# Half-width products and a written order of products around a chunked recurrence

## The chip, the cores and the metric

The kernel runs on one core of a Trainium2 chip. The metric is the time of one execution on the device in microseconds. The kernel before took 880.96 us (median of 3 runs, 880.44 to 882.03).

The core's engines each take their instructions in the order in which they stand in the engine's queue: PE (matrix products; PEld is its loading of weights), DVE and ACT (elementwise work), POOL (here it starts DMA transfers), and SP (which issues DMA transfers).

## The reference

One block of a streaming encoder for a sequence of 512 frames, width 1024, batch 1. An input projection feeds two branches whose gated sum is added to x; a cross-attention into a memory of 256 frames and a gated convolutional feed-forward network (FFN) follow.

```python
h = rms_norm(x, norm_mix_g[l])
proj = h @ w_in[l] + b_in[l]                       # 1024 -> 4864 columns
y_a = rwkv7_branch(proj[..., :cb0], ...) @ w_branch_a[l]
y_b = rglru_branch(proj[..., cb0:cb1], proj[..., cb1:cb2], ...) @ w_branch_b[l]
merged = sigmoid(proj[..., cb2:cg1]) * y_a + sigmoid(proj[..., cg1:]) * y_b
x = x + merged @ w_mix_out[l]
x = x + cross_attention(rms_norm(x, norm_x_g[l]), rms_norm(mem, norm_mem_g[l]), w_cq[l], w_ckv[l], w_co[l])
x = x + conv_ffn(rms_norm(x, norm_ffn_g[l]), w_ffn_in[l], ffn_conv_w[l], ffn_conv_b[l], w_ffn_out[l])

# the recurrence of rwkv7_branch: 8 heads of 64, state S (64 x 64) of each head
sa = S_{t-1} a_t;  S_t = S_{t-1} * w_t + sa b_t^T + v_t k_t^T;  y_t = S_t r_t
# rglru_branch: a = exp(8 * gate_a * log_sigmoid(lam)); h_t = a_t h_{t-1} + xb_t gate_x_t sqrt(1 - a_t^2)
```

## The kernel before

**Dense products.** Activations lie as [128 channels x 512 frames]. Each fp32 product is made of three products of rounded operands: high by high, high by low, low by high (`mm3`, L179, L180, L181). Weights arrive as tiles of 128 x 1024, eight blocks of 128 x 128 each, from the SP queue into four buffers (`win_r` and the like); ACT casts the high part (L122) and DVE subtracts for the low part (L123); high and low parts have three buffers each. `dense` takes one block of 128 output channels through its input blocks, three products each, over all 512 columns: 24 products for an in_ps, q, co or mix block (8 input blocks), 12 for a yb or ya block. In all 1680 products have 512 columns: 38 in_ps blocks, 8 each of mix, q and co, 8 each of yb and ya. The FFN uses products of 256 columns; its weights, and those for the memory's keys, lie 32 elements into their buffer (`OFF`).

**The scores of the recurrence.** For each pair of heads (0 to 3), `sc` (L691) multiplies rows of AK by rows of KBt, which DVE makes for each half of the partitions e = 0, 1 (L653, L654). Then follow `zh` and `zo`, small products of a triangular inverse, with copies of Hs between them.

**The recurrence** works through 8 chunks of 64 frames. In each chunk (`chunk`), PE makes 16 products x (state by AK); DVE copies x to Xs (L863); 16 first products of y; 16 of u from Xs; ACT and DVE each copy one half of u into UV (L875, L876); 16 products vr bring the next chunk's v into rows; 16 products s from UV and KBr make the new state, which DVE multiplies by decays into Sn (L892) and adds into the next UV (L896; for chunk 0 a copy, L898); SP (L903) is the decayed state for the step after; then 16 last products of y, and four transposes kbr bring the next KBr, copied by ACT (L848). So x of one chunk waits for UV of the chunk before, which waits for Sn, which waits for s.

**The RG-LRU branch** runs at the same time: `px_gates` takes in_ps14 to in_ps17, makes a convolution on DVE (L950), two gate products of 512 columns in plain fp32 (ga, gx; L954, L956) and activations on ACT; `px_scan` makes exp, ln and exp on ACT, then gx, xb and the scan on DVE (L969 to L972). ACT loads a table between kinds of function (L264). in_ps18 to in_ps21 give the gelu gate of this branch. `group_norm` normalizes the recurrence's output in two halves of 256 frames and two pairs of heads: products gv (sums of squares, L175, L176) and gg (the gate, L931), where for the first half gv and gg share one bank of the tag `rg`; DVE reads gg last in L936.

**What sets the order.** The tile framework schedules each engine's instructions by a model of costs, due times and priorities. The recurrence has the highest priority (`high_priority(offset=1000000)`). Dense products of in_ps16 to in_ps19 are placed by that scheduler between the recurrence's small products. The FFN's weights are partly summed in memory ahead of time by DMA transfers from POOL's queue (dS, dOs); `NSUM` says how many of these sums go out behind the products of an in_ps block (`sum_behind`).

`yb2`, the high and low part of the RG-LRU branch's output, lies in a buffer that held one half of hT, the normalized input that the in_ps products read.

Of the kernel before, what the change touches and what calls it, by code (L numbers as in the profile page):

```python
# [10 lines left out]
F32R = mybir.dt.float32r  # L11
# [6 lines left out]
P = 128  # L18
T = 512
# [4 lines left out]
HD = 64  # L24
# [14 lines left out]
IN_ORDER = IN_RWKV + IN_REST  # L39


PV_LAYOUT = [
    ("b_in", 38), ("mu", 14), ("w0", 4), ("a0", 4), ("k_k", 4), ("k_a", 4), ("r_k", 4),
    ("lnx_g", 4), ("lnx_b", 4), ("cbw", 16), ("cbb", 4), ("b_ga", 4), ("b_gx", 4), ("lam", 4),
# [14 lines left out]
def hybrid_block_kernel(ctx: ExitStack, tc: tile.TileContext, xT_d, mT_d, pv_d, cst_d, win_d, wk_d, wv_d,  # L59
                        lup_d, gup_d, rga_d, rgx_d, wba_d, wbb_d, wmix_d, wq_d, wo_d, wfi_d, wfo_d, out_d):  # L60
    nc = tc.nc
    V, S, PE = nc.vector, nc.scalar, nc.tensor

    wp = ctx.enter_context(tc.tile_pool(name="wp", bufs=3))
    cp = ctx.enter_context(tc.tile_pool(name="cp", bufs=1))
    big = ctx.enter_context(tc.tile_pool(name="big", bufs=1))
# [32 lines left out]
    OFF = 32  # L99
# [78 lines left out]
    def mm3(ps, lh, ll, rh, rl, start, stop, **kw):  # L178
        first = PE.matmul(ps, lh, rh, start=start, stop=False, **kw)  # L179
        PE.matmul(ps, lh, rl, start=False, stop=False, **kw)  # L180
        PE.matmul(ps, ll, rh, start=False, stop=stop, **kw)  # L181
        return first
# [112 lines left out]
    with tc.tile_pool(name="p0", bufs=1, reuse_waits="tile") as p0:  # L295
# [6 lines left out]
        o = PV["nmem"][0]  # L302
# [548 lines left out]
    def pc_b(c):  # L851
        return PC[:, :, c].unsqueeze(2).to_broadcast([P, NPAIR, HD])

    def chunk(c, UV, KBr, SP):
        last = c == NC - 1
        nUV = nKB = None
# [20 lines left out]
        if not last:  # L877
            nUV = rows_v(c + 1)
            pss = ch_ps(f"s{c}", "s")
            for j in range(NPAIR):  # L880
                for e in range(2):
                    PE.matmul(pss[half[e], j * HD:(j + 1) * HD], KBr[:, j, half[e]], UV[:, e, j, :],
                              start=True, stop=True)
# [61 lines left out]
    def px_gates(b):  # L945
        ps = inproj(14 + b)
        xb = tp.tile([P, T], F32, tag="xb", name=f"xb{b}", bufs=2)
        S.activation(xb, ps, AF.Identity, scale=par("cbw", 12 + b), bias=cbias[:, b:b + 1])
        for k in range(1, 4):
            V.scalar_tensor_tensor(xb[:, k:], ps[:, 0:T - k], par("cbw", 4 * (3 - k) + b), xb[:, k:],  # L950
                                   ALU.mult, ALU.add)
        V.tensor_tensor(xb[:, 0:3], xb[:, 0:3], ccor[:, :, b], ALU.subtract)
        psa = rw_ps(f"ga{b}", prg, tag="rg")
        PE.matmul(psa, rg[:, 0, b, :], xb, start=True, stop=True)  # L954
        psx = rw_ps(f"gx{b}", prg, tag="rg")
        PE.matmul(psx, rg[:, 1, b, :], xb, start=True, stop=True)  # L956
# [25 lines left out]
    for i in IN_REST[NMID:]:  # L982
        if i < 18:
            pair.append(px_gates(i - 14))
            if len(pair) == 2:
                for p in pair:
                    px_scan(*p)
                pair = []
        elif i < 22:
            if i == 19:  # L990
                for jp in range(2):
                    group_norm(0, jp, rw_ps(f"gv0_{jp}", prg, "rg"), rw_ps(f"gg0_{jp}", prg, "rg"))
            py_block(i - 18)
        else:
            gate_block(i - 22)
# [6 lines left out]
    pch_ctx.close()  # L1002


    yb2 = big.tile([P, 2, 4, T], F32R, tag="act16_0", name="yb2")
    mB = big.tile([P, KB, T], F32, tag="act16_1", name="mB")
    for b in range(4):
        yb = YB[:, b, :]
        with tc.high_priority():
            S.copy(yb2[:, 0, b, :], yb)  # L1010
            V.tensor_tensor(yb2[:, 1, b, :], yb, yb2[:, 0, b, :].bitcast(F32), ALU.subtract)
# [14 lines left out]
    ua = Units(wba_d, "wba")  # L1026
    for m in range(KB):
        ga = pm.tile([P, T], F32, tag="ga", name=f"gta{m}", bufs=5)
        nc.sync.dma_start(ga, dG[m])
# [84 lines left out]
    vs = load_kv("V", 0)  # L1114
    split_kv(vs[:1])
    vs = vs[1:] + load_kv("V", 1)
    uq = Units(wq_d, "wq")

    def q_head(hd, nsum=2):
        q2 = pk.tile([P, 2, 2, T], F32R, tag="q2", name=f"q2_{hd}", bufs=2)  # L1120
# [77 lines left out]
    uo = Units(wo_d, "wo", order)  # L1198
# [369 lines left out]
```

## Time and profile before

| | |
|---|---|
| median of 3 runs | 880.96 us (880.44 to 882.03) |
| profiled execution | 880.53 us, span 878.7 us |
| mean granted TensorE clock | 0.997 |
| busy: PE, PEld, DVE, ACT, POOL | 865.9, 756.0, 677.0, 514.0, 132.5 us |
| in_ps products of 512 columns | 304 each of three lines |
| recurrence, first vr to the group norm's first gg | 272.79 to 326.46 us |
| mix | 389.82 to 433.77 us |
| q and the attention, co, to the FFN's first product | 433.77 to 551.62 us |

How to read it: a timeline row gives start and duration in us, the engine, the line of the kernel, the operation, its output and inputs, the tile, and how many such instructions are put together; a square bracket gives the idle time before and what ended it. A matmul's duration overlaps that of the next, so a stream's pace is read from start to start. A group row gives total busy time, mean duration in ns, then idle time before the group's instructions. A window row gives its bounds, its length, then busy time and number of instructions of PE, PEld, DVE, ACT and POOL, the granted clock of PE, the DMA share and GB/s.

### The profile page before, as it was taken

The page shows a single profiled execution, that of the slowest core. Times are in us where ns is not written, and L with a number is a line of the kernel's source. Part 1 is how long each engine was busy: PE and PEld are TensorE (multiplying, and loading weights), DVE is VectorE, ACT ScalarE, POOL GpSimd, SP SyncE. Part 2 cuts the span into 40 slices and gives each one's busy share as a digit, 9 for nine tenths or more (in the row PEclk, how much of TensorE's full clock was granted, in tenths as well). Part 3 has the DMA queues.
Part 4 walks back from the last instruction along what each step waited for, and adds up shares of the span by engine and source line. Part 5 has one row for each costly group of instructions (what it writes and reads, how often), then busy time and mean ns, then how long its engine had stood idle before and what let it go on. Part 6 is the DMA issues. An engine that isn't in the chain of part 4 may idle for free.

```text
span 878.7 us, 15954 instructions
## 1 busy us (share of the span) xinstructions
PE 865.9 (99%) x6204; PEld 756.0 (86%) x6204; DVE 677.0 (77%) x1096; ACT 514.0 (58%) x788; POOL 132.5 (15%) x163
## 2 busy tenths in 40 slices
PE   9999999999999999999999999999999999999996
PEld 8878878888877677888887778999999999999996
DVE  6796598777976776685575568799888888999674
ACT  7576676634438576334454357666666566767563
POOL 0102222021101022001122211111111111111100
PEclk9999999999999999999999999999999999999998
DMA  8879899678997379758887968999989999998963
GB/s 288 283 272 222 204 226 234 198 187 248 265 231 164 77 183 243 201 177 228 223 238 176 198 150 192 263 265 282 295 256 296 294 283 292 257 286 210 305 183 95
DMA packets 97562, 201.37 MB, mean 229 GB/s; under 512 B 19600, under 2 KB 30992, under 8 KB 97424
## 3 DMA queue, kind: packets, MB, share of 16 engines
q1 hardware_dynamic: 62240, 118.57, 40.9%
q0 software_dynamic: 25504, 67.38, 37.4%
q10 hardware_dynamic: 9744, 14.42, 4.9%
q8 instruction: 48, 0.79, 0.4%
q14 instruction: 26, 0.21, 0.1%
HBM read 188.54 MB, written 78.12 MB: 303 GB/s over the span
## 4 chain that ended last, share of the span: by engine, by line
PE 89%; DVE 6%; DMA 2%; ACT 2%; issue 1%; DVEq 0%; ACTq 0%; SPq 0%
PE in_ps L180 7%; PE in_ps L181 7%; PE in_ps L179 7%; PE fx_ps L179 4%; PE fx_ps L181 4%; PE fx_ps L180 4%; PE fyz_ps L181 3%; PE fyz_ps L179 3%; PE fyz_ps L180 3%; PE oyz_ps L179 2%; PE oyz_ps L180 2%; PE oyz_ps L181 2%; PE q_ps L180 2%; PE co_ps L180 2%; PE mix_ps L181 2%; PE co_ps L179 2%
## 5 line engine op out<-in xcount | busy, mean ns | idle before, releaser
L145 ACT CAST wfi_h<-wfi_r 128x1024 fp32r<-128x1024 f32 x77 | 80.9, 1050 | 69.9 <-PE fyz_ps L180 24.4
L180 PE MATMUL in_ps<-hT,win_h 128*128 128x512 f32 x304 | 121.1, 398 | 0.4 <-DVE hT L396 0.4
L181 PE MATMUL in_ps<-hT,win_l 128*128 128x512 f32 x304 | 121.4, 399 | 0.0
L179 PE MATMUL in_ps<-hT,win_h 128*128 128x512 f32 x304 | 120.2, 397 | 0.3 <-DVE pr L598 0.3
L494 POOL DMA_DIRECT2D dS<-in_wfi x66 | 66.7, 1028 | 298.8 <-PE in_ps L179 101.1
L146 DVE TENSOR_TENSOR wfi_l<-wfi_r,wfi_h 128x1024 fp32r<-128x1024 f32 x77 | 94.2, 1223 | 22.5 <-ACT wfi_h L145 22.4
L180 PEld LDWEIGHTS in_ps<-hT,win_h 128*128 128x128 f32 x304 | 57.1, 188 | 14.7 <-DVE hT L396 1.1
L179 PEld LDWEIGHTS in_ps<-hT,win_h 128*128 128x128 f32 x304 | 57.1, 188 | 13.5 <-DVE pr L598 0.7
L181 PEld LDWEIGHTS in_ps<-hT,win_l 128*128 128x128 f32 x304 | 57.1, 188 | 12.6 <-issue 0.7
L530 POOL DMA_DIRECT2D dOs<-in_wfo x54 | 39.8, 789 | 170.3 <-PE fx_ps L179 46.7
L123 DVE TENSOR_TENSOR win_l<-win_r,win_h 128x1024 fp32r<-128x1024 f32 x38 | 46.3, 1221 | 24.1 <-ACT win_h L122 20.7
L122 ACT CAST win_h<-win_r 128x1024 fp32r<-128x1024 f32 x38 | 39.9, 1049 | 42.6 <-PE in_ps L180 32.6
L1379 DVE TENSOR_TENSOR wfo_l<-wfo_r,wfo_h 128x1024 fp32r<-128x1024 f32 (+1 forms) x39 | 47.4, 1217 | 12.6 <-ACT wfo_h L1378 12.6
L1378 ACT CAST wfo_h<-wfo_r 128x1024 fp32r<-128x1024 f32 (+1 forms) x39 | 40.4, 1035 | 25.3 <-DMA wfo_r<-dOs 10.0
L181 PE MATMUL ox_ps<-go,wfo_l 128*128 128x256 f32 x176 | 48.7, 277 | 0.7 <-DVE wfo_l L1379 0.7
L181 PE MATMUL fyz_ps<-hq,wfi_l 128*128 128x256 f32 x176 | 48.7, 277 | 0.3 <-DVE wfi_l L146 0.3
L179 PE MATMUL fyz_ps<-hq,wfi_h 128*128 128x256 f32 x176 | 48.8, 277 | 0.1
L179 PE MATMUL fx_ps<-hr,wfi_h 128*128 128x256 f32 x176 | 48.7, 277 | 0.0
L179 PE MATMUL fx_ps<-hq,wfi_h 128*128 128x256 f32 x176 | 48.6, 276 | 0.0
L180 PE MATMUL fx_ps<-hq,wfi_h 128*128 128x256 f32 x176 | 48.6, 276 | 0.0
L181 PE MATMUL fx_ps<-hq,wfi_l 128*128 128x256 f32 x176 | 48.6, 276 | 0.0
L180 PE MATMUL fyz_ps<-hq,wfi_h 128*128 128x256 f32 x176 | 48.6, 276 | 0.0
(432 smaller groups left out, 2694.9 us busy)
## 6 DMA issues: line engine op xcount, KB each, us to landing
dS<-in_wfi POOLq DMA_DIRECT2D x66, 512.0 KB, 7.6
wfi_r<-dS SPq DMA_DIRECT2D x44, 512.0 KB, 6.6
win_r<-in_win SPq DMA_DIRECT2D x38, 512.0 KB, 5.3
wfi_r<-in_wfi SPq DMA_DIRECT2D x33, 512.0 KB, 6.2
dS<-dS POOLq DMA_DIRECT2D x22, 512.0 KB, 5.6
dOs<-in_wfo POOLq DMA_DIRECT2D x12, 512.0 KB, 8.4
wk_r<-in_wk SPq DMA_DIRECT2D x8, 512.0 KB, 5.2
wv_r<-in_wv SPq DMA_DIRECT2D x8, 512.0 KB, 4.7
```

What stands on the lines that cost most here:

```text
L122: casts.append(S.copy(hi[:, o:o + n], raw[:, o:o + n]))
L123: V.tensor_tensor(lo[:, o:o + n], raw[:, o:o + n], hi[:, o:o + n].bitcast(F32), ALU.subtract)
L145: S.copy(hi, raw)
L146: V.tensor_tensor(lo, raw, hi.bitcast(F32), ALU.subtract)
L179: first = PE.matmul(ps, lh, rh, start=start, stop=False, **kw)
L180: PE.matmul(ps, lh, rl, start=False, stop=False, **kw)
L181: PE.matmul(ps, ll, rh, start=False, stop=stop, **kw)
L494: return lambda: nc.gpsimd.dma_start(s(out), src, **kw)
L530: yield lambda k=k, w=w, src=src: nc.gpsimd.dma_start(dO[n, m][:, k * P:(k + w) * P], src, **kw)
L1378: S.copy(hi[:, :n], raw[:, :n])
L1379: V.tensor_tensor(lo[:, :n], raw[:, :n], hi[:, :n].bitcast(F32), ALU.subtract)
```

## The change

- `dense` makes each product of 512 columns as two products of 256, for each of the three parts in turn; the 1680 products become 3360. The weights of these stages get the 32-element offset.
- `Products` records each product and transpose by the name of the tile it writes; at the end, `arrange` chains them by dependencies without a semaphore in the order of the list `ORDER`. A name with a number (`in_ps18:6`) takes so many products of the tile, a name alone the rest. The list covers in_ps4 to co_ps1. In it the recurrence's chunks 0 to 7 have no dense product between them until the last chunk (6 halves of in_ps18 before u7, 12 after); the gate products ga2, gx2, ga3, gx3 stand behind chunks 0 to 3; each `sc` is one piece of 16; gv0_1 follows gg0_0.
- Weight sums: 7 fewer behind in_ps17, in_ps18 and in_ps19, and 7 behind the last s product of chunks 0 to 6.
- `yb2` takes the buffer of tag `x16` (it held KBt) in place of that of hT.

```diff
+ORDER = """
...
+in_ps16 in_ps17:4 zo0 zh16 in_ps17:10 zo16 in_ps17:10 vr0 in_ps17 x0 y0:8 kbr0 u0 vr1 s0 y0 kbr1 ga2 x1 y1:8 u1
+vr2 s1 y1 kbr2 gx2 x2 y2:8 u2 vr3 s2 y2 kbr3 ga3 x3 y3:8 u3 vr4 s3 y3 kbr4 gx3 x4 y4:8 u4 vr5 s4 y4 kbr5 x5 y5:8
+u5 vr6 s5 y5 kbr6 x6 y6:8 u6 vr7 s6 y6 kbr7 x7 y7:8 in_ps18:6 u7 in_ps18:12 y7 in_ps18 in_ps19:24 gv0_0 in_ps19
+gg0_0 gv0_1 in_ps20:24 gg0_1 in_ps20 in_ps21 gv1_0 gg1_0 gg1_1 yb_ps0:18 yb_ps1:10 gv1_1 yb_ps1:8 yb_ps0 yb_ps1
...
-    V, S, PE = nc.vector, nc.scalar, nc.tensor
+    V, S = nc.vector, nc.scalar
+
+    class Products:
+
+        def __init__(self):
+            self.made = {}
+
+        def log(self, out, ins):
+            self.made.setdefault(out.tensor.source_name, []).append(ins.ins)
+            return ins
+
+        def matmul(self, out, *args, **kw):
+            return self.log(out, nc.tensor.matmul(out, *args, **kw))
...
+        def arrange(self, order):
+
+            last = None
+            for item in order:
+                name, _, n = item.partition(":")
+                tiles = [t for t in self.made if t == name or t.startswith(name + "_")]
+                left = sorted((i for t in tiles for i in self.made[t]), key=lambda i: int(i.name.split("-")[1]))
+                take = left[:int(n)] if n else left
+                for t in tiles:
+                    self.made[t] = [i for i in self.made[t] if i not in take]
+                for i in take:
+                    if last is not None:
+                        tc.add_manual_dep(i, last.name, mybir.DependencyInfo(
+                            mybir.DependencyClass.NoSync, mybir.DependencyReason.DATA), reason="order of products")
+                    last = i
+
+    PE = Products()
...
     def dense(ps, units, rhs, nkb, nsum=0):
 
+        n = min(ps.shape[-1], T // 2)
         for kb in range(nkb):
             wh, wl = units.next()
             rh, rl = rhs(kb)
-            ins = mm3(ps, wh, wl, rh, rl, kb == 0, kb == nkb - 1)
+            for o in range(0, ps.shape[-1], n):
+                ins = mm3(ps[:, o:o + n], wh, wl, rh[:, o:o + n], rl[:, o:o + n],
+                          kb == 0 and o == 0, kb == nkb - 1, skip_group_check=o > 0)
             if kb * nsum % nkb < nsum:
                 sum_behind(ins)
         return ins
...
-    uin = Units(win_d, "win")
+    uin = Units(win_d, "win", at=OFF)
...
-            37: 1, 17: 4, 18: 5, 19: 5, 20: 2, 21: 1}
+            37: 1, 17: 2, 18: 2, 19: 3, 20: 2, 21: 1}
...
+            paces.append(ins)
...
+            if i == 17:
+                for ins in paces:
+                    sum_behind(ins)
...
-    yb2 = big.tile([P, 2, 4, T], F32R, tag="act16_0", name="yb2")
+    yb2 = big.tile([P, 2, 4, T], F32R, tag="x16", name="yb2")
...
-    ub = Units(wbb_d, "wbb")
+    ub = Units(wbb_d, "wbb", at=OFF)
...
+    PE.arrange(ORDER)
```

Three places show how instructions move. On PE, around the fifth chunk of the recurrence before (in_ps are dense products, the others those of the chunks):

```order
L882 MATMUL s_2658<-UV_2570,KBr_2599 64x64 x8
L887 MATMUL y_2625<-BZ,UV_2570 64x64 x8
L835 MATMUL vr_2723<-cst,vT 64x64 x8
L181 MATMUL in_ps_3314<-hT_0_87,win_l_3318 128x512
L179 MATMUL in_ps_3314<-hT_0_87,win_h_3317 128x512
L860 MATMUL x_2690<-UV_2646,AK 64x64
L867 MATMUL y_2701<-AK,UV_2646 64x64
L180 MATMUL in_ps_3314<-hT_1_88,win_h_3317 128x512
L860 MATMUL x_2690<-UV_2646,AK 64x64 x7
L867 MATMUL y_2701<-AK,UV_2646 64x64 x7
```

The same place in the changed kernel (all products are recorded at L94 and transposes at L97):

```order
L94 MATMUL s_3234<-UV_3146,KBr_3175 64x64 x8
L94 MATMUL y_3201<-BZ,UV_3146 64x64 x8
L97 MATMUL kbr_3252<-cst,KBt 128x128 x4
L94 MATMUL x_3266<-UV_3222,AK 64x64 x8
L94 MATMUL y_3277<-AK,UV_3222 64x64 x8
```

Between s and the next x stood y, vr and dense products; now y and the transposes kbr stand there, and nothing of in_ps.

On DVE, in chunk 6 of the changed kernel, from Xs to the next chunk's UV (L921 is the copy to Xs, L934 that of u, L951 Sn, L955 the next UV; L1028 to L1031 are the RG-LRU branch's gx, xb and scan):

```order
L921 COPY Xs_3351<-x_3342 128x256
L1030 TENSOR_TENSOR xb_4023<-xb_4023,gx_4034 128x512
L1028 SCALAR_TENSOR_TENSOR gx_4108<-ga_4107,gx_4108 128x512
L934 COPY UV_3298<-u_1_3363 64x256
L1031 SCALAR_TENSOR_TENSOR YB<-ga_4033,xb_4023 128x512
L1029 MEMSET gx_4108 128x1
L1030 TENSOR_TENSOR xb_4097<-xb_4097,gx_4108 128x512
L951 TENSOR_TENSOR Sn_3410<-s_3386,PC 128x256
L1031 SCALAR_TENSOR_TENSOR YB<-ga_4107,xb_4097 128x512
L955 TENSOR_TENSOR UV_3374<-Sn_3410,SP_3338 64x256 x2
```

Before, the same instructions of this branch stood one chunk's copies apart in nearly the same way (one xb product and one scan between Xs and the copy of u, a second scan between Sn and UV); what differs is that PE has no dense products to make meanwhile.

On PE, in the group norm, first before, then now:

```order
L931 MATMUL gg_0_3355<-sgx,gup 128x256 x2
L179 MATMUL in_ps_3395<-hT_0_87,win_h_3398 128x512
L180 MATMUL in_ps_3395<-hT_1_88,win_h_3398 128x512
L181 MATMUL in_ps_3395<-hT_0_87,win_l_3399 128x512
```
```order
L94 MATMUL gg_0_4197<-sgx,gup 128x256 x2
L94 MATMUL gv_1_4217<-gv_1_h,bonesr 128x512
L94 MATMUL gv_1_4217<-gv_1_l,bonesr 128x512
L94 MATMUL in_ps_4299<-hT_0_87,win_h_4302 128x256
```

Ten dense products stood between gg_0 and gv_1; now none does.

More of the change, by code (lines that the diff above doesn't have):

```diff
@@ L39 @@
 IN_ORDER = IN_RWKV + IN_REST
+ORDER = """
+in_ps4 in_ps5 in_ps0 in_ps1 in_ps8 in_ps9 psw0 psa0 ss0 in_ps6 in_ps7 in_ps2:6 sc0 in_ps2:12 psw1 psa1 in_ps2:18
+ss1 in_ps2 in_ps3 in_ps10:30 sc1 in_ps10 in_ps11 psw2 psa2 ss2 in_ps22 in_ps23 in_ps24:6 sc2 in_ps24 psw3 psa3
+ss3 in_ps25 in_ps26 in_ps27:30 sc3 in_ps27 in_ps28 bo0 in_ps29 bo1 in_ps30 bo2 in_ps31 bo3 in_ps32 in_ps33
+in_ps34 in_ps35 in_ps36 in_ps37 in_ps14 in_ps15:42 ga0 in_ps15 in_ps16:2 gx0 in_ps16:38 ga1 in_ps16:6 zh0 gx1
+in_ps16 in_ps17:4 zo0 zh16 in_ps17:10 zo16 in_ps17:10 vr0 in_ps17 x0 y0:8 kbr0 u0 vr1 s0 y0 kbr1 ga2 x1 y1:8 u1
+vr2 s1 y1 kbr2 gx2 x2 y2:8 u2 vr3 s2 y2 kbr3 ga3 x3 y3:8 u3 vr4 s3 y3 kbr4 gx3 x4 y4:8 u4 vr5 s4 y4 kbr5 x5 y5:8
+u5 vr6 s5 y5 kbr6 x6 y6:8 u6 vr7 s6 y6 kbr7 x7 y7:8 in_ps18:6 u7 in_ps18:12 y7 in_ps18 in_ps19:24 gv0_0 in_ps19
+gg0_0 gv0_1 in_ps20:24 gg0_1 in_ps20 in_ps21 gv1_0 gg1_0 gg1_1 yb_ps0:18 yb_ps1:10 gv1_1 yb_ps1:8 yb_ps0 yb_ps1
+yb_ps2 yb_ps3 yb_ps4 yb_ps5 yb_ps6 yb_ps7 ya_ps0 ya_ps1 ya_ps2 ya_ps3 ya_ps4 ya_ps5 ya_ps6 ya_ps7 mix_ps0
+mix_ps1 mix_ps2 mix_ps3 mix_ps4 mix_ps5 mix_ps6 mix_ps7 q_ps0_0:32 rxc_ps q_ps0_0 q_ps0_1 q_ps1_0:24 sc_ps0_0
+sc_ps0_1 q_ps1_0 q_ps1_1:4 sc_ps0_2 prT_ps0:2 q_ps1_1:8 sc_ps0_3 prT_ps0:2 q_ps1_1:18 prT_ps0 q_ps1_1:10 o_ps0
+q_ps1_1 o_ps1 q_ps2_0:4 sc_ps1_0 sc_ps1_1 q_ps2_0:16 sc_ps1_2 prT_ps1:2 sc_ps1_3 prT_ps1:2 q_ps2_0:16 prT_ps1
+q_ps2_0:10 o_ps2 q_ps2_0 q_ps2_1:18 o_ps3 q_ps2_1 q_ps3_0:16 sc_ps2_0 sc_ps2_1 q_ps3_0:14 sc_ps2_2 prT_ps2:2
+sc_ps2_3 prT_ps2:2 q_ps3_0:16 prT_ps2 q_ps3_0 q_ps3_1:16 o_ps4 q_ps3_1:16 o_ps5 q_ps3_1 co_ps0:16 sc_ps3_0
+sc_ps3_1 co_ps0:14 sc_ps3_2 prT_ps3:2 sc_ps3_3 prT_ps3:2 co_ps0:6 co_ps4:10 prT_ps3 co_ps4:10 o_ps6 co_ps4:12
+o_ps7 co_ps4:4 co_ps0:6 co_ps4:6 co_ps0 co_ps4 co_ps1
+""".split()
 PV_LAYOUT = [
@@ L61, in hybrid_block_kernel, with transpose @@
     nc = tc.nc
-    V, S, PE = nc.vector, nc.scalar, nc.tensor
+    V, S = nc.vector, nc.scalar
[7 more added lines that the diff above has]
+            return self.log(out, nc.tensor.matmul(out, *args, **kw))
+        def transpose(self, out, *args):
+            return self.log(out, nc.tensor.transpose(out, *args))
+        def arrange(self, order):
[13 more added lines that the diff above has]
+    PE = Products()
     wp = ctx.enter_context(tc.tile_pool(name="wp", bufs=3))
@@ L852, in pc_b @@
         return PC[:, :, c].unsqueeze(2).to_broadcast([P, NPAIR, HD])
+    paces = []
     def chunk(c, UV, KBr, SP):
@@ L881, in chunk @@
                 for e in range(2):
-                    PE.matmul(pss[half[e], j * HD:(j + 1) * HD], KBr[:, j, half[e]], UV[:, e, j, :],
-                              start=True, stop=True)
+                    ins = PE.matmul(pss[half[e], j * HD:(j + 1) * HD], KBr[:, j, half[e]], UV[:, e, j, :],
+                                    start=True, stop=True)
+            paces.append(ins)
         for j in range(NPAIR):
@@ L1116, in hybrid_block_kernel @@
     vs = vs[1:] + load_kv("V", 1)
-    uq = Units(wq_d, "wq")
+    uq = Units(wq_d, "wq", at=OFF)
     def q_head(hd, nsum=2):
@@ L1197, in hybrid_block_kernel @@
     order = [0, 4, 1, 5, 2, 6, 3, 7]
-    uo = Units(wo_d, "wo", order)
+    uo = Units(wo_d, "wo", order, at=OFF)
     for m in order:
```

4 lines of the change are left out of this document (2 added, 2 removed).

## The prediction

> **What bounds the kernel now.** I read the page's busy times first and then its chain of waits: TensorE (PE) works in 99% of the span and carries 89% of the chain that ends last. Time is therefore won or lost where the pace of PE's products changes, or where PE waits.
>
> ```profile
> PE 865.9 (99%) x6204; PEld 756.0 (86%) x6204; DVE 677.0 (77%) x1096; ACT 514.0 (58%) x788; POOL 132.5 (15%) x163
> PE 89%; DVE 6%; DMA 2%; ACT 2%; issue 1%; DVEq 0%; ACTq 0%; SPq 0%
> ```
>
> The 6% of DVE and 2% of ACT are mostly the recurrence. I read next the windows of the recurrence (272.79 to 326.46), the part of in_ps alone in it, and a purely dense stage, the mix.
>
> ```profile
> 272.79:326.46 53.67, 53.27 (x844) 38.88 (x843) 39.90 (x80) 38.30 (x72) 8.17 (x9) 1.00 0.58 134
> 272.79:326.46 53.67, 17.49 (x49) 8.09 (x48) 4.48 (x6) 2.23 (x3) 1.00 0.58 134
> 389.82:433.77 43.95, 43.95 (x194) 36.06 (x192) 25.39 (x32) 17.39 (x25) 7.47 (x8) 1.00 0.82 211
> ```
>
> PE shows no idle time in the first window, but 48 in_ps products and 2 of the group norm lie in it by program order (the second row counts 49 records, overlapping): 50 dense ones, at the mix's pace of 43.95/192 = 0.229 us worth 11.45 us. The recurrence itself, with four gate products, thus costs 53.67 - 11.45 = 42.2 us net. The granted clock is 1.00 in all these rows.
>
> **The change part by part.** (1) *Halves.* A product of 512 columns against one of 256, start to start, from the first and last row of a run of 45 and of a run of 51 intervals:
>
> ```profile
> 84.67 0.39 PE L179 MATMUL in_ps<-hT,win_h 128*128 128x512 f32 x1
> ...
> 94.97 0.39 PE L179 MATMUL in_ps<-hT,win_h 128*128 128x512 f32 x1
> ```
> ```profile
> 599.99 0.28 PE L179 MATMUL fyz_ps<-hq,wfi_h 128*128 128x256 f32 x1
> ...
> 605.77 0.28 PE L179 MATMUL fyz_ps<-hr,wfi_h 128*128 128x256 f32 x1
> ```
>
> 10.30/45 = 0.2289 and 5.78/51 = 0.1133; two halves take 0.2267, 2.1 ns less. 1680 products are split (912 of in_ps, 192 each of mix, q and co, 96 each of yb and ya): 1680 x 2.1 ns = **-3.5 us**. The FFN's rows already have the weights at the 32-element offset that the others get now, so I take its pace; the bounds are 0 (the smaller product gains only there) and -4. The number of weight loads doubles, and the FFN rows pay for the same number.
>
> The Trainium skill says otherwise: its page "TensorE: Matmul & The Clock Gate", section "Back-to-back issue gap", gives N/2.4 + 2.5 ns per product, so that halving would add 2.5 ns to each of 1680, an estimate of +4.2 us in place of -3.5. By that rule halves always cost; the two runs of rows above disagree with it (0.2267 against 0.2289).
>
> (2) *The recurrence in one piece.* One chunk before, on PE, and what DVE and ACT do for it:
>
> ```profile
> 298.97 0.69 PE L882 MATMUL s<-UV,KBr 128*64 128x64 f32 x16
> 299.58 0.67 PE L887 MATMUL y<-BZ,UV 64*64 64x64 f32 x14
> 300.19 1.12 PE L954 MATMUL ga<-xb,rg 128*128 128x512 f32 x2
> 301.24 0.69 PE L860 MATMUL x<-UV,AK 128*64 128x64 f32 x16
> 301.76 0.64 PE L867 MATMUL y<-AK,UV 128*64 128x64 f32 x16
> 302.32 0.33 PE L847 MATMUL kbr<-cst,KBt 128*128 128x128 f32 x1
> 302.58 0.68 PE L873 MATMUL u<-Xs,BZ 64*64 64x64 f32 x16
> 303.19 0.55 PE L847 MATMUL kbr<-cst,KBt 128*128 128x128 f32 x3
> 303.58 1.02 PE L956 MATMUL gx<-xb,rg 128*128 128x512 f32 x2
> 304.53 0.69 PE L882 MATMUL s<-UV,KBr 128*64 128x64 f32 x16
> ```
> ```profile
> 299.70 0.42 DVE L892 TENSOR_TENSOR Sn<-s,PC 128x256 f32<-128x256 f32 x1 [0.21 <-PE s L882]
> 300.16 0.87 DVE L896 TENSOR_TENSOR UV<-Sn,SP 64x256 f32<-64x256 f32 x2
> 301.06 0.87 DVE L903 TENSOR_TENSOR SP<-UV,PC 64x256 f32<-64x256 f32 x2
> 301.97 0.42 DVE L863 COPY Xs<-x 128x256 f32<-128x256 f32 x1
> 303.34 0.43 DVE L876 COPY UV<-u 64x256 f32<-64x256 f32 x1 [0.94 <-PE u L873]
> ```
>
> What is gained: dense products between small ones cost more than their 0.229 us.
>
> ```profile
> 276.34 0.50 PE L179 MATMUL in_ps<-hT,win_h 128*128 128x512 f32 x1
> 276.77 0.51 PE L873 MATMUL u<-Xs,BZ 64*64 64x64 f32 x10
> ```
>
> Here one occupies 0.43, so about 0.2 us goes with each place at which PE changes over; before has some 25 such places, 5 us. What is lost: the dense products had filled the waits. The chain without them, by the rows above: from s to the next x 0.69 + 0.42 + the first half of UV 0.43 and three gaps of 0.04 = 1.7 us, which y (0.61) and kbr (four, about 0.4) nearly fill, or 2.6 where a gate product (0.95) stands there too; from x to u 1.2 (0.69 + 0.42), or 1.8 where SP (0.87) stands before Xs on DVE; from u to s 1.25 (0.68 + 0.43, or vr's 0.61 behind u). That is 5.1 for a chunk with a gate product (0 to 3), 4.6 for 4 to 6, and 5.2 for the last, whose gaps hold 18 halves: 4 x 5.1 + 3 x 4.6 + 5.2 = 39.4. Less the halves (18 x 0.1133 = 2.0) and with the first vr (0.8), 38.2 net against 42.2, a gain of 4 if nothing else stood on DVE and ACT.
>
> But other work stands there, in order, with these lengths (groups of DVE, then ACT, within the recurrence):
>
> ```profile
> L972 DVE TENSOR_TENSOR_SCAN YB<-ga,xb 128x512 f32<-128x512 f32 x4 | 4.9, 1223 | 0.1
> L971 DVE TENSOR_TENSOR xb<-xb,gx 128x512 f32<-128x512 f32 x4 | 2.8, 692 | 0.2
> L969 DVE SCALAR_TENSOR_TENSOR gx<-ga,gx 128x512 f32<-128x512 f32 x4 | 2.8, 690 | 3.1 <-ACT gx L265 3.1
> L123 DVE TENSOR_TENSOR win_l<-win_r,win_h 128x1024 fp32r<-128x1024 f32 x2 | 2.4, 1220 | 0.0
> ```
> ```profile
> L264 ACT ACT_TABLE_LOAD x4 | 5.1, 1283 | 0.1
> L122 ACT CAST win_h<-win_r 128x1024 fp32r<-128x1024 f32 x2 | 2.1, 1049 | 0.3 <-PE in_ps L180 0.3
> ```
>
> I put the order of the changed DVE and ACT instructions beside these lengths, chunk by chunk, each starting when its inputs and its engine allow. Chunk 0: before the copy of u stand xb's product (0.69) and win_l (1.22), which waits for a table load (1.28) and the cast (1.05) on ACT; before Sn stand a scan (1.22) and an xb step: +2.5. Chunks 1 and 2: xb steps, and a tanh ahead of ACT's copy: +1.3. Chunks 3 to 5: +1.0. Chunk 6 again holds two xb products, two scans and a gx step around the copy of u and Sn, and a table load on ACT: +2.7. Sum +7.5. Lengths from x0 to the last y: 7.6, 5.8, 5.7, 5.3, 4.7, 5.3, 7.4, 5.2 = 47.0; less 2.0, with 0.8: 45.8 against 42.2, **+3.6**. Bounds: -4 when all of this slips beside the chain, +6 when a further scan and a table load (2.5) end last. I take the sum, because these engines take their instructions in order; laid out in the same way, before's stretch comes out within about 1 us of its trace.
>
> (3) *Group norm.* gv0_1 now follows gg0_0 at once, and both use one bank; gg0_0 is read until DVE's last step ends:
>
> ```profile
> 326.46 1.02 PE L931 MATMUL gg<-sgx,gup 128*128 128x256 f32 x4
> ```
> ```profile
> 328.64 0.69 DVE L936 TENSOR_TENSOR vT<-y,gg 128x512 f32<-128x512 f32 x1
> ```
>
> Before, ten dense products (2.3 us) fill the time to 329.33. Now PE waits: **+1.0** (bounds 0 and +2.2, the whole of 329.33 - 327.13). What is late is in_ps20 behind gv0_1 on PE's queue.
>
> (4) *Scores.* A set of 16 now runs in one piece and needs the rows of both halves at once:
>
> ```profile
> 133.50 0.69 DVE L653 TENSOR_TENSOR KBt<-kk,L 64x512 f32<-64x512 f32 x1
> 134.11 0.68 DVE L654 TENSOR_TENSOR KBt<-pk,L 64x512 f32<-64x512 f32 x1
> ```
> ```profile
> 117.88 0.50 PE L620 MATMUL psw<-pwa,lhi 128*128 128x512 f32 x1 [0.40 <-ACT BZ L698]
> 133.73 1.16 PE L691 MATMUL sc<-AK,KBt 64*128 64x128 f32 x8
> ```
>
> The eight products at 133.73 wait until 134.79 in the new form. Over four scores I take 2.0 of such waits, less psw's 0.4 and two changeovers of 0.2: **+1.2** (0 to +2.8). Small products zo behind copies of Hs, placed in the same way: **+0.3**.
>
> (5) *yb2 in another buffer.* The wait at yb goes with most of its changeover; gv1_1 now waits some 0.4 between the yb products:
>
> ```profile
> 345.95 0.50 PE L180 MATMUL yb_ps<-yb,wbb_h 128*128 128x512 f32 x1 [0.41 <-DVE yb L1011]
> ```
>
> **-0.2** (bounds -0.6 and +0.4). (6) *Weight sums.* Seven move from dense products to the s products of the chunks.
>
> ```profile
> dS<-in_wfi POOLq DMA_DIRECT2D x66, 512.0 KB, 7.6
> ```
>
> Their number is unchanged, the DMA share in the recurrence is 0.58, and what they feed, the FFN, starts 225 us after the recurrence: 0. Without that cover one landing of 7.6 us would be late. The attention's new order places products about as the trace has them: 0, within 1 either way.
>
> Sum: -3.5 + 3.6 + 1.0 + 1.2 + 0.3 - 0.2 = **+2.4**. The profiled execution took 880.53 (878.7 of span and 1.8 around it), so 882.9; the median of the runs is 0.43 higher: **883.4**.
>
> **The rivals.** *Slack on DVE and ACT takes half of the delay* (what (2) gains in changeovers pays the rest): recurrence about -0.1, all else as above, -1.3: 879.7. For it: before, DVE idles while it waits for u (0.94 us at 303.34). Against: in chunks 0 and 6 the queues before the copy are longer than such gaps. *The chain runs at its own pace*: recurrence -4, sum -5.2: 875.8. For it: DVE is busy 39.90 and ACT 38.30 of the window's 53.67 us, so that work spread evenly would just fit beside the chain; against: the chain's 39.4 is no longer than that, so nothing may stand in the wrong place. *Halves gain nothing outside the FFN* (slower): if a weight load or a bank's handover between halves takes back the 2.1 ns, which would decide in every dense stage, the sum is +5.9: 886.9. For it: two loads now stand where one did. Against: the FFN's pace. By the rule of the Trainium skill named above this case would come to an estimate of 891.1. That the change does not do what it says I exclude for PE: its listed order is the one the list of tiles asks for.
>
> **How the numbers follow.** Forecast 0.48, half of the delay 0.27, own pace 0.17, halves for nothing 0.08. Two per mille, 1.8 us, is about what the runs can tell from no change: 879.2 to 882.7. The own-pace case and the lowest parts of the half-delay one (0.08) are faster: 0.25; the rest of that and the lower end of the forecast (0.10) are the same: 0.29; what remains, 0.46, is slower. The forecast's own range, by the bounds of (2) to (4), is 881 to 887. Held to 8 in 10 with the own-pace case: 876.0 to 887.5.
>
> **What would show it.** Products of 256 in in_ps, mix, q and co start 0.1133 apart; the mix takes 43.5 us instead of 43.95. From x0 to the last y lie about 47 us, with PE waiting for the copies of u and for Sn in chunks 0 and 6, over 2 us each. About 1 us before gv0_1 is put down to DVE. The forecast is wrong if these waits stay under 1 us each (then it is near 876), or if the half products start over 0.1145 apart (then it is near 887).

## The result, and the profile after

The changed kernel takes 885.88 us (median of 4 runs, 885.61 to 887.02) against 880.7 for the kernel before beside it: ratio 1.0064, 95% interval 1.0051 to 1.0076, slower by 5.2 us by the medians. The profiled execution has a span of 885.2 us against 878.7; it was the slowest of the four, 1.1 us over the median, so the stages below add up to more than 5.2.

Of the changed kernel's page, the busy times and the engines of the chain that ended last:

```profile
PE 856.7 (97%) x7884; PEld 826.7 (93%) x7884; DVE 679.4 (77%) x1096; ACT 514.1 (58%) x788; POOL 132.5 (15%) x163
PE 72%; DVE 14%; ACT 6%; DMA 5%; issue 3%; DVEq 0%; ACTq 0%; SPq 0%
```

PE is busy 97% instead of 99%, and its part of the chain fell from 89% to 72%: most of what was added is waiting for DVE and ACT. The windows from the first vr to the first gg, of the mix, and of q, attention and co:

```profile
273.78:334.54 60.76, 52.98 (x915) 44.71 (x915) 41.15 (x82) 38.12 (x72) 11.65 (x13) 0.97 0.60 140
395.83:439.85 44.02, 43.80 (x387) 43.60 (x386) 25.51 (x33) 17.56 (x24) 7.47 (x8) 1.00 0.81 213
439.85:558.41 118.56, 116.53 (x954) 112.27 (x953) 79.86 (x171) 62.82 (x122) 21.23 (x23) 1.00 0.78 192
```

Before, PE was idle for 0.40 us of the first (53.27 busy of 53.67, which the prediction read as no idle time) and not at all in the other two; the third of before was

```profile
433.77:551.62 117.85, 117.85 (x569) 94.17 (x568) 78.88 (x171) 62.62 (x123) 21.27 (x23) 1.00 0.80 193
```

And within the mix, two rows with 174 half products between them:

```profile
414.01 0.39 PE L94 MATMUL mix_ps<-mg,wmix_h 128*128 128x256 f32 x2
...
433.73 0.39 PE L94 MATMUL mix_ps<-mg,wmix_h 128*128 128x256 f32 x2
```

19.72/174 = 0.1133: the halves run as the FFN's products do, 2.2 ns less for each former product (0.2289 - 0.2267). To see where time went, I take from each stage its dense products at their pace (0.2289 a product, 0.1133 a half) and compare the rest. From the first in_ps to the first vr the rest grew by 2.9 us, from there to gg by 4.5, from gg to yb (group norm) by 1.1, from yb to q by 0.6 (0.5 of it at the head of the mix, at a wait for its input), from q to the FFN by 1.6; the FFN and its end are 0.3 shorter, the start 0.1. That is +10.2, and -3.7 for the halves: +6.5, the difference of the spans.

The waits that carry it (PE's waits in the changed kernel; total, times, longest):

```profile
PE s L94 <- DVE UV L934: 2.7, 5, 0.9
PE x L94 <- DVE UV L955: 1.9, 1, 1.9
PE in_ps L94 <- DVE pr L654: 1.6, 1, 1.6
PE s L94 <- ACT UV L933: 1.5, 2, 0.8
PE sc L94 <- ACT kk L693: 1.2, 2, 0.6
```

The longest is in chunk 6. DVE's timeline there, and what PE shows:

```profile
314.01 0.43 DVE L934 COPY UV<-u 64x256 f32<-64x256 f32 x1
314.47 1.23 DVE L1031 TENSOR_TENSOR_SCAN YB<-ga,xb 128x512 f32<-128x512 f32 x1
...
315.75 0.69 DVE L1030 TENSOR_TENSOR xb<-xb,gx 128x512 f32<-128x512 f32 x1
316.48 0.42 DVE L951 TENSOR_TENSOR Sn<-s,PC 128x256 f32<-128x256 f32 x1
316.82 1.21 DVE L1031 TENSOR_TENSOR_SCAN YB<-ga,xb 128x512 f32<-128x512 f32 x1
317.95 0.84 DVE L955 TENSOR_TENSOR UV<-Sn,SP 64x256 f32<-64x256 f32 x2
```
```profile
318.40 1.07 PE L94 MATMUL x<-UV,AK 128*64 128x64 f32 x15 [1.93 <-DVE UV L955]
```

s is done at 315.3, yet Sn starts at 316.48, behind a scan and an xb step, and UV behind a second scan. Three windows from there on (the number before the DMA share is the granted clock):

```profile
318.00:320.00 2.00, 1.48 (x33) 1.26 (x33) 1.88 (x5) 0.00 (x0) 0.00 (x0) 0.96 1.04 158
320.00:322.00 2.00, 2.00 (x15) 1.78 (x16) 0.00 (x0) 0.00 (x0) 0.53 (x1) 0.50 1.02 253
322.00:324.00 2.00, 2.00 (x22) 1.88 (x20) 0.43 (x1) 0.36 (x1) 0.19 (x1) 0.69 0.83 209
```

After this wait PE's clock falls to half for 3.4 us (319.84 to 323.26), in the last chunk.

### The profile page after: what moved, and what is told of

Read it like the earlier page. It is cut to its first block, busy times and chain, and to the rows that moved or that the text cites. A ratio compares the mean times of both kernels' runs of the same rounds, so it can differ in the third digit from the quotient of the medians.

```text
span 885.2 us, 19309 instructions
## 1 busy us (share of the span) xinstructions
PE 856.7 (97%) x7884; PEld 826.7 (93%) x7884; DVE 679.4 (77%) x1096; ACT 514.1 (58%) x788; POOL 132.5 (15%) x163
## 4 chain that ended last, share of the span: by engine, by line
PE 72%; DVE 14%; ACT 6%; DMA 5%; issue 3%; DVEq 0%; ACTq 0%; SPq 0%
PE fx_ps L94 14%; PE in_ps L94 13%; PE fyz_ps L94 10%; PE ox_ps L94 6%; PE co_ps L94 5%; PE mix_ps L94 4%; PE q_ps L94 4%; PE oyz_ps L94 3%; PE yb_ps L94 2%; DVE win_l L176 2%; PE v_ps L94 2%; DMA wfo_r<-dOs 1%; PE o_ps L94 1%; PE k_ps L94 1%; PE sc_ps L94 1%
## 5 line engine op out<-in xcount | busy, mean ns | idle before, releaser
L94 PE MATMUL in_ps<-hT,win_h 128*128 128x256 f32 x1216 | 213.5, 280 | 2.0 <-DVE pr L654 1.6
L94 PEld LDWEIGHTS in_ps<-hT,win_h 128*128 128x128 f32 x1216 | 185.5, 188 | 5.7 <-DVE pr L654 1.8
L94 PE MATMUL in_ps<-hT,win_l 128*128 128x256 f32 x608 | 169.4, 279 | 0.6 <-DVE win_l L176 0.6
L94 PEld LDWEIGHTS in_ps<-hT,win_l 128*128 128x128 f32 x608 | 114.6, 189 | 1.9 <-DVE win_l L176 1.0
L94 PE MATMUL fx_ps<-hq,wfi_h 128*128 128x256 f32 x352 | 61.2, 276 | 0.0
L94 PE MATMUL fx_ps<-hr,wfi_h 128*128 128x256 f32 x352 | 61.1, 276 | 0.0
L94 PE MATMUL fyz_ps<-hq,wfi_h 128*128 128x256 f32 x352 | 61.1, 276 | 0.0
L94 PE MATMUL ox_ps<-go,wfo_h 128*128 128x256 f32 x352 | 60.0, 276 | 0.0
L1441 DVE TENSOR_TENSOR wfo_l<-wfo_r,wfo_h 128x1024 fp32r<-128x1024 f32 (+1 forms) x39 | 47.1, 1211 | 12.5 <-ACT wfo_h L1440 10.3
L94 PEld LDWEIGHTS fx_ps<-hq,wfi_h 128*128 128x128 f32 x352 | 53.2, 188 | 0.0
L94 PEld LDWEIGHTS fx_ps<-hr,wfi_h 128*128 128x128 f32 x352 | 53.0, 188 | 0.2 <-ACT sn L1376 0.2
L94 PEld LDWEIGHTS ox_ps<-go,wfo_h 128*128 128x128 f32 x352 | 53.0, 188 | 0.0
L94 PEld LDWEIGHTS fyz_ps<-hq,wfi_h 128*128 128x128 f32 x352 | 53.0, 188 | 0.0
L94 PE MATMUL ox_ps<-go,wfo_l 128*128 128x256 f32 x176 | 48.7, 277 | 0.7 <-DVE wfo_l L1441 0.7
L94 PE MATMUL fyz_ps<-hq,wfi_l 128*128 128x256 f32 x176 | 48.7, 277 | 0.6 <-DVE wfi_l L199 0.6
```

What stands on the lines that cost most here:

```text
L94: return self.log(out, nc.tensor.matmul(out, *args, **kw))
L1441: V.tensor_tensor(lo[:, :n], raw[:, :n], hi[:, :n].bitcast(F32), ALU.subtract)
```

## The experiments

Theory at the start: the halves gain about 3.7 us wherever they stand, and the written order loses more than that, in the recurrence (4.5), the group norm (1) and the attention (1.6). Ratios are to the kernel before, run beside each.

**Halves alone.** The kernel before with the new `dense` and the offset, no written order.

> The kernel before with only the half-width products and the weights' offset; the scheduler orders all products. Theory (halves gain 2.1 to 2.3 ns for each of 1680, the written order loses): 880.7 - 3.7 = 877, between 876 and 879. Rival (halves themselves bring the loss, by waits they make or by what the scheduler does with twice as many products): 883 or more.

904.61 us, ratio 1.0255 (1.0234 to 1.0276). The theory missed by 27.6 us. PE's waits in this run:

```profile
PE yb_ps L179 <- DVE mB L1021: 3.7, 1, 3.7
PE sc L694 <- DVE KBt L657: 2.9, 5, 0.9
PE in_ps L181 <- DVE win_l L123: 2.9, 5, 0.8
```

They lie in several of the mixed stages. The scheduler had remade the order of all engines for products of another size, so this run does not show the halves' own worth. It shows that the written order is not to be measured against the order of before: with halves and no written order the kernel is 19 us slower than with it.

**The written order with products of 512 columns** (`n = ps.shape[-1]`, counts of dense pieces halved).

> The changed kernel with its written order and paced sums, but products of 512 columns (the counts in the order halved, so that each piece holds the same work). Theory: the order alone costs what the change costs plus what the halves gain, 885.9 + 3.7 = 889.6, between 888.5 and 890.5. Rival (halves cost or give nothing here): 886 or less.

896.81 us, ratio 1.0178 (1.0159 to 1.0196): 7.2 over the theory. It reaches the first vr when the kernel before does (272.87 us against 272.79); then PE, DVE and ACT are in another relation, and this is the longest wait, with the clock behind it:

```profile
PE ga L93 <- DVE xb L1010: 4.5, 1, 4.5
```
```profile
280.00:286.00 6.00, 1.80 (x36) 1.43 (x36) 5.88 (x12) 2.94 (x6) 0.70 (x1) 0.86 0.72 218
286.00:292.00 6.00, 5.34 (x68) 3.61 (x70) 3.40 (x8) 2.12 (x4) 0.00 (x0) 0.57 0.00 0
```

More of the 7.2 us lies in the pace. In the mix, 84 products of 512 columns lie between these two rows:

```profile
411.75 0.62 PE L93 MATMUL mix_ps<-mg,wmix_h 128*128 128x512 f32 x2
...
431.21 0.62 PE L93 MATMUL mix_ps<-mg,wmix_h 128*128 128x512 f32 x2
```

19.46/84 = 0.2317, 2.8 ns more than the 0.2289 of before, worth 4.7 us for 1680 products. What the dense stages of this run have different from before is the weights' offset of 32 elements; the offset alone was not run. So by this run it isn't the offset that makes the halves faster: with the offset a full product takes longer, not less.

The parts of the change are not additive: order and size were fitted to each other.

**The recurrence left to the scheduler**, the rest of the written order kept:

```diff
-in_ps16 in_ps17:4 zo0 zh16 in_ps17:10 zo16 in_ps17:10 vr0 in_ps17 x0 y0:8 kbr0 ...
+in_ps16 in_ps17:4 zo0 zh16 in_ps17:10 zo16 in_ps17:10 [ vr0 in_ps17 x0 y0:8 kbr0 ...
...
-gg0_0 gv0_1 in_ps20:24 gg0_1 in_ps20 in_ps21 gv1_0 gg1_0 gg1_1 yb_ps0:18 ...
+gg0_0 gv0_1 in_ps20:24 gg0_1 in_ps20 in_ps21 gv1_0 gg1_0 gg1_1 ] yb_ps0:18 ...
```

(items between the brackets are counted but not chained).

> The changed kernel, but the order of products from the first vr to the last gg is left to the scheduler, which puts dense halves between the small products again. Theory (PE has nothing to do while it waits for DVE and ACT in the one-piece chunks, 4.5 us, and before gv0_1, 1 us): 885.9 - 5.5 = 880.4, between 879 and 882. Rival (the waits are set by DVE's and ACT's queues whatever PE does): 884 or more.

880.62 us, ratio 0.9998 (0.9987 to 1.0008). As the theory has it: vr to yb takes 47.4 us beside its dense products, against 47.1 before and 52.6 in the changed kernel. PE fills the time with halves. The run doesn't show this alone, for DVE's order moved with it: the last two scans stand in chunks 5 and 6, one each, where the changed kernel has both in chunk 6. But the kernel before has both in chunk 6 too, with dense products beside them.

**The attention left to the scheduler** (the list ends at mix_ps7).

> The changed kernel with its written order only up to the mix; q, the attention and co are left to the scheduler. Theory (the four new waits of 0.4 to 0.55 us at sc_ps and o_ps go): 885.9 - 1.6 = 884.3. Rival (those waits are moved work and cost nothing, or fewer changeovers pay for them): 885.5 to 886.5.

888.69 us, ratio 1.0077 (1.0062 to 1.0093): slower than the changed kernel, where both readings had it the same or faster. The intervals of the two overlap, but the stage itself tells them apart: from q to the FFN the rest is 33.8 us instead of 31.5. For halves the written order of the attention is better than the scheduler's; it is worse only beside what full products had.

**Halves in the order of before.** Written down for PE from the kernel before, counts of dense pieces doubled; sums and yb2's buffer as before.

> The kernel before (its sums and its buffer of yb2 too) with half-width products, and with its own order of products on PE written down: each dense piece has twice as many halves at the same place. Theory (halves gain about 2.2 ns for each of 1680 where PE never waits; the run with halves alone lost its time through the order that the scheduler made for them): 880.8 - 3.7 = 877, between 876 and 879.5, since a few waits on DVE may come earlier. Rival (halves cost by themselves in the mixed stages, so that before's order loses too): 883 or more.

886.09 us, ratio 1.0069 (1.0057 to 1.0081). The theory missed again. The largest wait, in the otherwise dense stage before the recurrence:

```profile
PE in_ps L124 <- DVE win_l L206: 2.5, 4, 0.9
```

DVE's order had moved: a cast of low weights stood two instructions of the triangular inverse later than its counterpart before. DVE in this run, then in the kernel before:

```profile
227.74 0.76 DVE L849 TENSOR_TENSOR zz<-Zt,Nm 128x576 f32<-128x576 f32 x1
228.42 1.22 DVE L206 TENSOR_TENSOR win_l<-win_r,win_h 128x1024 fp32r<-128x1024 f32 x1
```
```profile
225.81 0.71 DVE L763 TENSOR_TENSOR zz<-Zt,Nm 128x529 f32<-128x529 f32 x1
226.43 1.22 DVE L123 TENSOR_TENSOR win_l<-win_r,win_h 128x1024 fp32r<-128x1024 f32 x1
```

**gv0_1 apart from gg0_0**: `gg0_0 in_ps20:20 gv0_1 in_ps20:16 gg0_1`.

> The changed kernel with 20 halves of in_ps20 between gg0_0 and gv0_1 (and 16 in place of 24 before gg0_1). Theory (the wait of 0.97 us for the last reader of the shared bank goes, one changeover of 0.2 comes): 885.9 - 0.8 = 885.1. Rival (what follows gv0_1, gg0_1, then waits as long): 885.9.

884.42 us, ratio 1.0045 (1.0033 to 1.0057): 1.5 less than the changed kernel. The wait before gv0_1 is gone, and from gg to yb the rest falls from 5.5 to 4.3 us. The spans of the two profiled executions differ by more, 2.6 us, and the other 1.4 isn't the edit's: the same wait in chunk 6 stands here, but this time PE's clock stayed at 1.00 behind it, and the last chunk, from x to the start of the last y, took 4.64 us instead of 6.06.

```profile
319.37 1.07 PE L94 MATMUL x<-UV,AK 128*64 128x64 f32 x15 [1.93 <-DVE UV L955]
...
324.01 0.68 PE L94 MATMUL y<-BZ,UV 64*64 64x64 f32 x16
```

**Sums and buffer undone** (`NSUM` as before, no sums behind the chunks, yb2 in `act16_0`).

> The changed kernel with the weight sums counted as before (none behind the chunks) and yb2 in the buffer of hT again. Theory: the sums cost nothing (within 0.4) and the buffer's wait of 0.4 us at yb may come back: 885.9 to 886.4. Rival (seven sums in the recurrence slow its transfers, or the sums behind too few products come late for the FFN): 884.5 or less.

887.11 us, ratio 1.0075 (1.0063 to 1.0087). The wait for yb is back, with more than twice the time it had before (0.41):

```profile
PE yb_ps L94 <- DVE yb L1070: 1.0, 1, 1.0
```

The intervals of this run and of the changed kernel overlap. The buffer's wait is seen; sums and buffer are not told apart beyond that.

**Scans late.** The last two gx steps, and with them the xb steps and scans that need them, held behind the last chunk's copy of u:

```diff
-        V.scalar_tensor_tensor(gx, ga, 1.0, gx, ALU.add, ALU.mult)
+        ins = V.scalar_tensor_tensor(gx, ga, 1.0, gx, ALU.add, ALU.mult)
+        if b > 1:
+            tc.add_manual_dep(ins.ins, copied[-1].ins.name, mybir.DependencyInfo(
+                mybir.DependencyClass.NoSync, mybir.DependencyReason.DATA), reason="scan behind the chunks")
```

> The changed kernel with the last two gx steps, xb steps and scans of the RG-LRU branch held on DVE until the last chunk's copy of u. Theory (chunk 6 is 7.5 us long because two scans of 1.22 us and the steps before them stand ahead of the copy of u, Sn and the next UV): its length falls to about 5, the whole by 2.3 to 883.6, between 883 and 884.4. Rival (the table load on ACT, or the chain itself, sets chunk 6): 885.3 or more.

882.15 us, ratio 1.0021 (1.0012 to 1.003): 3.7 less, more than the 2.3 expected. Chunk 6, from x to x, falls from 7.51 to 5.29 us, as the theory has it:

```profile
309.66 0.98 PE L94 MATMUL x<-UV,AK 128*64 128x64 f32 x15
314.95 1.00 PE L94 MATMUL x<-UV,AK 128*64 128x64 f32 x15
...
319.51 0.68 PE L94 MATMUL y<-BZ,UV 64*64 64x64 f32 x16
```

The other 1.5 us is the last chunk: from x to the start of the last y 4.56 instead of 6.06 us, at a clock of 1.00:

```profile
316.00:318.00 2.00, 2.00 (x39) 1.74 (x33) 0.43 (x1) 0.00 (x0) 0.56 (x1) 1.00 0.95 122
```

So one idle piece of 1.93 us cost itself and 1.5 us more through the clock. That this is the clock, and not the scans' absence from the last chunk, is shown by the run with gv0_1 apart, which has the scans in their old place, the same wait, and 4.64 us at a clock of 1.00.

**Halves with every order of before.** As the run in PE's order of before, but DVE's and ACT's order is written down too, instruction by instruction; with that, only the width and the weights' offset differ.

> As the run with half-width products in the order of the kernel before, but the orders of DVE and ACT are written down too, instruction by instruction as in the kernel before; so the products' width is all that differs. Theory (the 886 of that run came from casts of weights that the scheduler put later on DVE once the products were halved, four waits of 0.5 to 0.9 us in a stage that is otherwise dense): the waits go and the halves' gain shows, 880.5 - 3.7 = 876.8, between 875.5 and 878.5. Rival (halves need the low part of the weights 0.23 us sooner, or cost elsewhere by themselves): 881 or more.

887.18 us, ratio 1.0067 (1.005 to 1.0083). The theory fell a third time: the waits for win_l are gone, and others stand in their place. In this kernel all instructions of ACT and DVE are recorded at L194, PE's products at L221. ACT, then PE, then three windows of this run; last, ACT's cast in the kernel before:

```profile
266.11 1.04 ACT L194 CAST win_h<-win_r 128x1024 fp32r<-128x1024 f32 x1 [2.33 <-PE in_ps L221]
```
```profile
267.81 1.18 PE L221 MATMUL zo<-BZ,Hs 32*32 32x32 f32 x60 [1.61 <-ACT Hs L194]
```
```profile
262.00:268.00 6.00, 4.38 (x87) 3.04 (x88) 1.51 (x2) 2.53 (x4) 0.00 (x0) 1.00 0.34 140
268.00:274.00 6.00, 6.00 (x188) 5.71 (x186) 3.03 (x6) 4.25 (x6) 1.14 (x1) 0.63 0.40 101
274.00:280.00 6.00, 6.00 (x59) 5.59 (x54) 0.69 (x1) 2.14 (x5) 0.72 (x1) 0.52 0.89 202
```
```profile
264.04 1.04 ACT L122 CAST win_h<-win_r 128x1024 fp32r<-128x1024 f32 x1
```

The cast writes over the high weights of an older block and waits for their last reader. With 512 columns a block ends with one product of low weights, which alone stood behind gx. With the halves taken one after the other (three products of the first half, three of the second) the last two products stand there, and one of them reads the high weights. So the cast, the copy of Hs behind it on ACT and zo behind that came 2 us late, PE stood idle for 1.61 us, and its clock was half for ten (269.55 to 279.79). The clock didn't fall so in every execution: two of the six have a mean clock of 0.997 and 0.998 and took 885 us; the profiled one has 0.993 and took 888.53.

**Halves in pairs.** That reading says what to change: let each part of the operands be needed first, and let go last, at the same product as before.

```diff
-            for o in range(0, ps.shape[-1], n):
-                ins = mm3(ps[:, o:o + n], wh, wl, rh[:, o:o + n], rl[:, o:o + n],
-                          kb == 0 and o == 0, kb == nkb - 1, skip_group_check=o > 0)
+            for k, (w, r) in enumerate(((wh, rh), (wh, rl), (wl, rh))):
+                for o in range(0, ps.shape[-1], n):
+                    one = PE.matmul(ps[:, o:o + n], w, r[:, o:o + n], start=kb == k == o == 0,
+                                    stop=kb == nkb - 1 and k == 2, skip_group_check=o > 0)
+                    ins = one if k == 0 else ins
```

> As the run with halves and all orders of the kernel before, but the two halves of each product stand side by side (high by high of both halves, high by low of both, low by high of both), so that each part of the operands is needed first, and let go last, at the same product as before. Theory (halves gain 2.2 ns each of 1680; what they lost in that run came from the order within a block: low parts of weights and of activations needed 0.23 and 0.11 us sooner, the last reading of the high part of the weights one product later, so that a cast on ACT waited, PE stood idle for 1.6 us and its clock fell): no wait over that of before, clock 1.00 in the recurrence, 881 - 3.7 = 877.3, between 876 and 878.5. Rival (smaller products lose at every place where PE changes over or waits, whatever their order): 881 or more.

878.09 us (877.38 to 879.66), ratio 0.9974 (0.9965 to 0.9984): faster than both kernels. The same window as above, and PE's waits:

```profile
268.00:274.00 6.00, 5.70 (x111) 5.05 (x109) 1.70 (x4) 4.88 (x9) 2.38 (x3) 1.00 0.94 201
```
```profile
PE yb_ps L221 <- DVE yb L194: 0.4, 1, 0.4
PE psw L221 <- ACT BZ L194: 0.4, 1, 0.4
```

These are the waits of before. The order of the six products within a block was the loss of the run with every order of before: it is all that differs between the two, and they are 9 us apart (7 where the clock didn't fall). Of the 10.6 us between their traces, 5.6 lie from bo to the first gg, where the late cast is; 2.9 lie in the attention and co, where the waits are others.

Of the 3.7 us by the pace, the median gains 2.3. In this pair of traces the stages with halves gain less, 1.3, since up to the FFN those that mix small and dense products take 2.4 us more beside their halves, in many small pieces whose cause the runs don't show; the other 1.2 lies in the start and the FFN, which have no part in the edit.

**Late scans and gv0_1 apart together.**

> The changed kernel with both edits, the late scans and the 20 halves between gg0_0 and gv0_1. Theory (the two terms are in different places and add): 885.9 - 3.7 - 1.5 = 880.7, between 879.8 and 881.6, equal to the kernel before. Rival (the scans now stand before the group norm's steps on DVE, so that gv0_1 waits anyway): 882.

881.56 us, ratio 1.0006 (0.9998 to 1.0015), within what was expected. The 1.5 for gv0_1 held a part of the clock's share, which the late scans' 3.7 hold already; with 1.2 in its place, the sum is 881.0. With these two edits of its order the changed kernel is as fast as the kernel before, with the recurrence still in one piece.

**The change with halves in pairs**, all its own orders written down.

> The changed kernel with its own orders of PE, DVE and ACT written down, and only the two halves of each product put side by side. Theory (outside the recurrence and the group norm the change loses partly by the order within a block: two waits for low weights of 0.6 us together, one of 0.4 in the mix, some 0.5 in the attention): 885.9 - 1.5 = 884.4, between 883.5 and 885.2. Rival A (all that the change loses outside the recurrence and the group norm, some 4 us, is of this kind): 882 or less. Rival B (the written order was made for halves of one part after the other, so nothing is gained): 885.6 or more.

884.98 us, ratio 1.0043 (1.0029 to 1.0058), in the range expected, though not by the waits named: the mix is 0.2 shorter, attention and co 0.3, but the waits for low weights stand there still (0.8 in all, 0.6 without this edit). The gain of 0.9 lies within overlapping intervals: in the changed kernel the order within a block costs about 1 us by these medians, against 9 in the orders of before.

## Why the prediction was right, point by point

The direction and the recurrence's mechanism were right; of the size, 5.2 us, the prediction had 2.4. What it lacked by the traces are +1.9 in the stretch before vr, +1.6 in the attention, +0.9 in the recurrence (the clock) and +0.5 in the mix; the scores came out 0.6 cheaper.

*Halves, -3.5.* The rows of the prediction give 2.2 ns, not 2.1, and so -3.7; the measured pace gives the same, so the term holds. The rule that each product costs a fixed addition, which spoke for +4.2 (the Trainium skill, "TensorE: Matmul & The Clock Gate", section "Back-to-back issue gap", which gives it for an isolated product), does not hold for these products: 0.1133 twice is less than 0.2289, and halves in pairs are 2.3 us faster as a whole. What the step left out is that a product's size also decides when operands are needed and let go: alone, halves cost 6 us in before's orders, and 24 with the scheduler's. The mix, forecast at 43.5 us, took 44.0, since waits at its head took back what the pace gave.

*Recurrence, +3.6.* Chunk lengths from x0 were laid out as 7.6, 5.8, 5.7, 5.3, 4.7, 5.3, 7.4; measured 7.42, 5.48, 5.62, 5.22, 4.76, 5.04, 7.50, in sum 0.8 less. The stretch cost +4.5. What the term left out is the clock: for the last chunk 5.2 was laid out at full clock, and it ran partly at half clock, 1.4 us that are missing in the trace of gv0_1 apart, where the stretch cost +3.0. So the price of the queues themselves was put a little too high, and the clock hid it. The run with late scans shows the cause (DVE takes the scans in order, before Sn and UV) and the price of chunk 6: 2.2, against 2.3 expected of that run and 2.7 in the prediction. PE's waits were forecast as over 2 us in chunks 0 and 6 each; they are 1.2 and 3.0.

*Group norm, +1.0.* The wait is 0.97, and the stage grew by 1.1.

*Scores, +1.2 with zo 0.3.* The four new waits sum to 2.0 us, as taken, but from the first sc to the first bo the rest grew by 0.1 only, though a wait for pr rose there from 0.30 to 1.56; that fewer changeovers pay for more than I counted is likely, but no run shows it alone. From the first in_ps to the first sc it grew by 0.5. Between bo and vr it grew by 2.2, where I had only the 0.3 of zo: low parts of weights that come late cost 1.3 from start to start (0.6 of it as two waits), and from zo to vr 0.6.

*yb, -0.2.* +0.13 from yb to ya; with sums and buffer undone the wait is 1.0, not the 0.4 of before.

*Sums, 0.* The run without the new sums doesn't contradict it, nor does it show it alone.

*Attention, 0.* This step failed: +1.6, four waits of 0.4 to 0.55 us at sc_ps and o_ps that before did not have. The order of products there was compared by places, not laid out against DVE's queue as in the recurrence.

The rival "own pace" fell by the waits; "half of the delay" by the chunk lengths. "Halves gain nothing" named 886.9, nearer to 885.9 than the forecast of 883.4, but by chance: the halves start 0.1133 apart, and what came on top lies elsewhere.

## What to carry to other kernels

When a product is split, keep for every operand the place of its first and its last reader: the pace of the pieces is only half of the account, and a cast that waits one product longer held up ACT and, behind it, PE. Filling PE's queue with small dependent products is safe only as far as the queues of the engines that answer them are free of long work in the wrong place; lay those queues out too, as far as the order is written by hand. An order of one engine that a scheduler made is fitted to the order of the others: changing the size of the work, or one engine's order, moves them all, so an edit is measured alone only when all of them are held, as in the three runs with all orders written down.

## What was not expected of the hardware

An idle piece of PE below 2 us can be enough for its clock to fall, and the same piece need not be: after the 1.93 us of chunk 6 the clock was half in the changed kernel and stayed full with gv0_1 apart. After 1.61 us it was half for ten (halves with every order of before); after a single wait of 2.12 us, before gv in the run with 512 columns, it stayed full. So it isn't the length of one idle piece.

What the traces show is a fixed grid of time. In the changed kernel the clock first becomes full at 5.82 us (the first products start 0.427 us apart up to there and 0.227 from there on) and falls at 319.84, 92 times 3.413 us later. In all fourteen traces the half clock begins a whole number of such steps after the first full clock, and inside the kernel it lasts one, two or three of them (3.41, 6.83, 10.24). What goes with a fall is how little PE did in the step before it. The changed kernel, then gv0_1 apart, where the same idle piece of 1.93 us reaches 0.2 us past the end of a step:

```profile
316.43:319.84 3.41, 1.36 (x33) 1.18 (x32) 3.27 (x7) 0.68 (x2) 0.29 (x1) 1.00 0.89 172
319.84:323.26 3.42, 3.42 (x29) 2.99 (x27) 0.58 (x2) 0.36 (x1) 0.72 (x1) 0.50 0.98 228
```
```profile
312.31:315.72 3.41, 2.28 (x67) 2.04 (x69) 3.25 (x7) 3.35 (x7) 0.00 (x0) 1.00 0.89 111
315.72:319.14 3.42, 1.72 (x36) 1.35 (x33) 3.34 (x6) 1.56 (x4) 1.15 (x1) 1.00 0.94 209
```

In these traces every step with PE busy for less than 1.6 us was followed by half clock, and of the fuller ones only two: 1.67 us at the changed kernel's end, and 1.79 us of mostly 32x32 products with every order of before. The clock's first rise, and with it the grid, lies anywhere from 4.41 to 7.05 us into these traces, so whether an idle piece costs the clock too is partly luck.

The Trainium skill ("TensorE: Matmul & The Clock Gate", section "Part 1: The HAM clock gate (the "warmup" mystery)") names an idle window of about 3.4 us as what brings the clock to half. The half and the 3.4 us agree with these traces; that the window must be idle does not, since PE was busy for 1.36 of 3.41 us here.
